# Delta-rule layer: exponentials and norm factors spread over partitions by way of DRAM, one pool limit for two kinds of tiles, keys ahead of queries

## The chip, the cores and the metric

The kernel runs on one core of a Trainium2 chip. The metric is the device time of one execution in microseconds (us). An execution is profiled by the hardware; the profile's span runs from the first to the last instruction.

## What is computed

One inference step of a 4-layer hybrid encoder for 512 prompt rows and 64 sample rows (576 columns in all) of width 1024. Layer 0 mixes by pooling, layer 1 by a gated delta rule, layer 2 by stick-breaking attention, layer 3 by pooling again, and a feed-forward part with a short causal convolution stands behind each mixer. The change touches the delta-rule layer alone:

```
qkv, z, a, b = split(h @ w_in); qkv = silu(causal_dwconv(qkv))          # 8 heads, head size 128
q = l2norm(q) * DK**-0.5; k = l2norm(k); beta = sigmoid(b)
g = -exp(a_log) * softplus(a + dt_bias)                                 # decay, one number per head and row
gc = cumsum(g) within a chunk
m = (k*beta) @ k.T * exp(gc_i - gc_j) below the diagonal                # per chunk and head
u, w = triangular_solve(I + m, [v*beta, k*beta*exp(gc)])
attn = (q @ k.T) * exp(gc_i - gc_j); qg = q * exp(gc); kg = k * exp(gc_last - gc)
for each chunk: v_new = u - w @ s; o = qg @ s + attn @ v_new; s = s*exp(gc_last) + kg.T @ v_new
o = rmsnorm(o, norm_w) * silu(z);  y = o @ w_out
```

## The kernel before, in words

All instructions go through a small planner. Each piece of work is a generator (a task) with a priority; it yields the tiles, buffers or events that it needs, and the planner, with a cost for each instruction and a due time for each tile, picks which task goes on. What comes out is one fixed order per engine, and every engine, the queue SP that issues all DMAs too, works in this program order. So an instruction that waits holds everything behind it on its engine. Since one helper issues everything, all rows of the profile bear the line L26; tiles are told apart by their names (a, b, d, h, p, q, r, t are pools of buffers; p is PSUM; dn_... are constants of this layer).

In the delta layer (`dn`) the planner has these tasks, for each of 8 heads:

- projections: for k, q, v and z of every head 48 matmuls (128x288, weights split in a high and a low part) on PE, in the order that the string `order` of the table TN gives (`k4` is the key of head 4). `conv` follows a k, q or v: POOL writes three columns of the old state ahead of the data and copies the last three columns out, DVE multiplies and adds, ACT takes tanh, DVE adds.
- `mat(h)`: the gram matrix of the key (PE), its diagonal (DVE), a power for the key's norm (POOL), decay factors by a small matmul (`bank`) and exponential (ACT), the product M (DVE), and seven stores of M to DRAM (SP). M has the class 'M', of which two tiles may be alive.
- `inverse(g)`: the triangular inverses of 32x32 blocks for four heads at a time, 31 steps of two POOL instructions. Group 0 waits for the matrices of heads 0 to 3, group 1 for those of heads 4 to 7.
- `merge(h)`: loads inverse blocks from DRAM, puts them together to U (class 'U', two tiles alive).
- `prep_rec(h)`: the masked products of q and k, and eg, the exponential of the cumulated decay of head h on all 128 partitions: `bank(h,None)` on PE (two matmuls, weights dn_idr) and two exponentials on ACT.
- `rec(h)`: the recurrence over the chunks, head after head. At its end the output o is normed: squares (ACT), sums over partitions (PE, ten matmuls with ones), a factor r[128,5] (DVE, then a power on POOL), the spread of these 576 factors over 128 partitions by five matmuls (ten instructions) against the identity (c_ident,t), and two multiplications (DVE, a<-p,dn_nw,a).
- `z_post(h)` multiplies o by silu(z), and the output projection (weights h, moving data b) takes all eight heads.

Of the kernel before, what the change touches and what calls it, by code (L numbers as in the profile page):

```python
# [9 lines left out]
F32 = mybir.dt.float32  # L10
F32R = mybir.dt.float32r
BF16 = mybir.dt.bfloat16
AF = mybir.ActivationFunctionType
ALU = mybir.AluOpType
# [22 lines left out]
class Flow:  # L37
# [213 lines left out]
TN={'mat': 2,  # L251
 'inv': 3,
 'merge': 5,
 'prep': 10,
 'rec': 2,
 'cv': 6,
 'M': 2,
 'tu': 4,
 'tu_': 2,
 'mg': 3,  # L260
 'U': 2,
 'v': 2,
 'vs': 2,
 'pr': 4,
# [7 lines left out]
 'pv': 4,  # L272
 'pz': 6,
 'w': 8,
 'order': 'k0 q0 q1 k1 k2 q2 k3 q3 v2 v0 v1 v3 k4 q4 k5 k6 q6 k7 q5 q7 z1 z0 z2 z3 v5 v4 v6 v7 z4 z5 z7 z6',
 'pa': 3,
 'pb': 2,
 'pc': 7,
# [11 lines left out]
class Step:  # L290
# [890 lines left out]
    def dn(self,l,st,nst,gnext):  # L1181
        nc=self.nc; I=self.I; O=self.O; mm=self.E.matmul; T_=self.E.transpose; V=self.V; A=self.A; G=self.G; S=self.S; f=self.f
# [5 lines left out]
        nw=c1([128,1],"nw"); mhalf=c1([128,5],"mhalf"); idr=c1([128,8],"idr",F32R)  # L1188
        cst=c1([128,3],"cst"); mc=c1([128,1],"mc")
        tok=c1([128,5,72],"tok")  # L1190
        bE=c1([128,5,8],"bE"); ngc=c1([128,5,8],"ngc"); beta=c1([128,5,8],"beta"); nbe=c1([128,5,8],"nbe"); ekg=c1([128,5,8],"ekg")
        gh=[None]
        cc=[slice(128*c,128*c+128) for c in range(4)]; sm=slice(512,576); ss=slice(SO,SO+64)
        blocks=[(128*b,128*b+128) for b in range(4)]+[(512,576)]
        def prep():
# [15 lines left out]
        def ab_post(P):  # L1211
            rb=self.rb[st]
            yield [f"{st}:rb0",f"{st}:rb1"]
            f.free(self.acc[st])
            yield [("a",3)]
            Yt=self.a(); t_=self.a(); Ft=self.a()
            Y=Yt[:40,:NT]; t=t_[:40,:NT]; F=Ft[:,:NT]
            self.lnexp()
            A.activation(mc[:40],cst[:40,2:3],AF.Exp)
            V.tensor_scalar(out=mc[:40],in0=mc[:40],scalar1=-1.0,scalar2=None,op0=ALU.mult)  # L1220
            G.memset(F,0.0)
            yield [P[0],P[1],rb[:,:NT]]
            for h,p in enumerate(P):
                a,b=HALF[h]
                V.tensor_tensor(out=Y[:,a:b],in0=p[:40,:HW],in1=rb[:40,a:b],op=ALU.mult)
            f.free(*P)
            V.tensor_scalar(out=Y,in0=Y,scalar1=cst[:40,0:1],scalar2=cst[:40,1:2],op0=ALU.mult,op1=ALU.add)
            yield [Y]
            A.activation(t,Y,AF.Abs)
            A.activation(t,t,AF.Exp,scale=-1.0)  # L1230
            A.activation(t,t,AF.Ln,bias=self.one[:40])
            yield [t]
            V.scalar_tensor_tensor(out=Y,in0=Y,scalar=0.0,in1=t,op0=ALU.max,op1=ALU.add)
            V.tensor_scalar(out=Y,in0=Y,scalar1=mc[:40],scalar2=None,op0=ALU.mult)
            V.tensor_copy(F[32:40],Y[32:40])
            for a,b in blocks:
                V.tensor_tensor_scan(out=F[0:8,a:b],data0=self.ones[0:8,:b-a],data1=Y[0:8,a:b],initial=0.0,op0=ALU.mult,op1=ALU.add)
                V.tensor_scalar(out=F[64:72,a:b],in0=F[0:8,a:b],scalar1=F[0:8,b-1:b],scalar2=-1.0,op0=ALU.subtract,op1=ALU.mult)
            yield [("a",1)]
            g=gh[0]=self.a(F32R)  # L1240
            G.memset(g[:,:NT].bitcast(F32),0.0)
            V.tensor_copy(g[0:8,:NT],F[0:8])
            V.tensor_tensor(out=g[32:40,:NT],in0=F[0:8],in1=g[0:8,:NT].bitcast(F32),op=ALU.subtract)
            f.free(Yt,t_)
            yield [F,("p",1)]
            p=self.p()
            for i,(a,b) in enumerate(blocks): T_(p[:b-a,72*i:72*i+72],F[0:72,a:b],self.ident[:72,:72])
            yield [p]
            V.tensor_copy(tok[:,0:4],p[:,:288].rearrange("p (a b) -> p a b",b=72))
            V.tensor_copy(tok[:64,4],p[:64,288:360])  # L1250
            f.free(p,Ft)
            V.tensor_tensor(out=bE,in0=tok[:,:,0:8],in1=tok[:,:,32:40],op=ALU.add)
            V.tensor_scalar(out=ngc,in0=tok[:,:,0:8],scalar1=-1.0,scalar2=None,op0=ALU.mult)
            yield [bE]
            A.activation(beta,tok[:,:,32:40],AF.Exp)
            A.activation(nbe,bE,AF.Exp)
            A.activation(ekg,tok[:,:,64:72],AF.Exp)
            yield [ekg]
            V.tensor_scalar(out=beta,in0=beta,scalar1=0.5,scalar2=None,op0=ALU.mult)
            V.tensor_scalar(out=nbe,in0=nbe,scalar1=-1.0,scalar2=None,op0=ALU.mult)  # L1260
            f.fire(f"{st}:dec")
# [109 lines left out]

        def mat(h):
            k=kq[h][:,0]
            yield [k[:,:579],("a",1,"M"),("p",2),("t",1)]
            M=self.a(cls="M"); r=self.s([128,5],F32,"t",8)
            p=self.p(); q=self.p()
            G.memset(r,1.0)
            for c in range(4): mm(p[:,cc[c]],k[:,cc[c]],k[:,cc[c]],start=True,stop=True)
            mm(q[:64,:64],k[:,ss],k[:,ss],start=True,stop=True)
            yield [p,q[:64,:64],r,"@V"]  # L1380
            for c in range(4): V.scalar_tensor_tensor(out=M[:,cc[c]],in0=p[:,cc[c]],scalar=1.0,in1=self.ident,op0=ALU.mult,op1=ALU.mult,accum_out=r[:,c:c+1])
            V.scalar_tensor_tensor(out=M[:64,sm],in0=q[:64,:64],scalar=1.0,in1=self.ident[:64,:64],op0=ALU.mult,op1=ALU.mult,accum_out=r[:64,4:5])
            V.tensor_scalar(out=r,in0=r,scalar1=4e-6,scalar2=None,op0=ALU.add)
            V.reciprocal(out=rk2[:,h],in_=r)
            G.tensor_tensor(out=r,in0=r,in1=mhalf,op=ALU.pow)
            yield [f"{st}:dec",("p",1)]
            p2=self.p()
            G.memset(M[64:128,sm],0.0)
            bank(h,self.mpos,p2,q,64)
            yield [r,rk2[:,h]]  # L1390
            V.tensor_tensor(out=nbk[:,h],in0=nbe[:,:,h],in1=rk2[:,h],op=ALU.mult)
            V.tensor_tensor(out=vsc[:,h],in0=beta[:,:,h],in1=r,op=ALU.mult)
            f.free(r)
            f.fire(f"{st}:kn{h}")
            yield [p2,q[:64,64:128],"@A"]
            for c in range(4): A.activation(M[:,cc[c]],p2[:,cc[c]],AF.Exp,scale=-1.0,bias=bE[:,c,h:h+1])
            A.activation(M[:64,sm],q[:64,64:128],AF.Exp,scale=-1.0,bias=bE[:64,4,h:h+1])
            f.free(p2)
            yield [M[:,:NT],"@V"]
            for c in range(4): V.scalar_tensor_tensor(out=M[:,cc[c]],in0=p[:,cc[c]],scalar=rk2[:,h,c:c+1],in1=M[:,cc[c]],op0=ALU.mult,op1=ALU.mult)  # L1400
            V.scalar_tensor_tensor(out=M[:64,sm],in0=q[:64,:64],scalar=rk2[:64,h,4:5],in1=M[:64,sm],op0=ALU.mult,op1=ALU.mult)
            f.free(p,q)
            g=h//4; o=18*(h%4)
            if g not in dM: dM[g]=self.dram([72,32,32])
            d=dM[g]
            yield [M[:,:NT]]
            for b in range(4):
                S.dma_start(out=d[o:o+16].rearrange("(c b) i j -> b i c j",b=4)[b],
                    in_=M[32*b:32*b+32,:512].rearrange("p (c j) -> p c j",j=128)[:,:,32*b:32*b+32])
            for b in range(2): S.dma_start(out=d[o+16+b],in_=M[32*b:32*b+32,512+32*b:544+32*b])  # L1410
            Mt[h]=self.dram([128,NT]); S.dma_start(out=Mt[h],in_=M[:,:NT])
            f.free(M)
            f.fire(f"{st}:M{h}")
# [90 lines left out]
        def prep_rec(h):  # L1504
# [3 lines left out]
            yield [("a",2,"pr"),("a",1,"eg"),("p",2),("d",1,"ks"),("t",1)]  # L1508
            at=self.a(cls="pr"); eg=self.a(cls="eg"); kg=self.a(cls="pr"); kgs=self.d("ks")[:64]; gl=self.s([128,5],F32,"t",8)
            p=self.p(); q=self.p()  # L1510
            bank(h,self.mneg,p,q,0)
            yield [p,q,"@A"]
            for c in range(4): A.activation(at[:,cc[c]],p[:,cc[c]],AF.Exp,bias=ngc[:,c,h:h+1])
# [4 lines left out]
            yield [p,q,"@V"]  # L1518
            V.tensor_tensor(out=at[:,:512],in0=p,in1=at[:,:512],op=ALU.mult)
            V.tensor_tensor(out=at[:64,sm],in0=q[:64,:64],in1=at[:64,sm],op=ALU.mult)  # L1520
            yield [at]
            bank(h,None,p,q,0)
            yield [p,q,"@A"]
            A.activation(eg[:,:512],p,AF.Exp)
            A.activation(eg[:,sm],q[:,:64],AF.Exp)
            yield [eg]
            for b in range(4): T_(p[:,cc[b]],k[:,cc[b]],self.ident)
            T_(q[:64,:128],k[:,ss],self.ident)
            G.tensor_copy(gl[:,0:4],eg[:,127:512:128]); G.tensor_copy(gl[:,4:5],eg[:,575:576])
# [9 lines left out]
        def rec(h):  # L1539
# [7 lines left out]
            for c in (4,0,1,2,3):  # L1547
# [3 lines left out]
                if s is not None:  # L1551
                    yield [s,ks,("p",1),("d",1,"rr")]
                    p=self.p()
# [42 lines left out]
            sq=self.a(cls="eg")  # L1596
            A.activation(sq[:,:NT],o[:,:NT],AF.Square)
            q=yield from sums(sq,512)
            f.free(sq)
            yield [("t",1)]  # L1600
            r=self.s([128,5],F32,"t",8)
            V.scalar_tensor_tensor(out=r,in0=q[:,:5],scalar=1.0/128,in1=eq[:,h],op0=ALU.mult,op1=ALU.add)
            G.tensor_tensor(out=r,in0=r,in1=mhalf,op=ALU.pow)
            yield [r,("p",1)]
            p=self.p()
            for i in range(4): mm(p[:,cc[i]],r[:,i:i+1].to_broadcast([128,128]),self.ident,start=True,stop=True)
# [8 lines left out]
        def z_post(h):  # L1615
# [25 lines left out]
                dno[h]=t  # L1641
                f.fire(f"{st}:o{h}")
            return g
        f.lim.update({k:TN[k] for k in ('cv','M','tu','tu_','mg','U','v','vs','pr','eg','ks','o_','S','rr')})
        def k_(h):
            if h: proj(8+h,qk_post(h,0),TN['pk'])
            else: first(qk_post(0,0))
# [390 lines left out]
```

## Time and profile before

| | |
|---|---|
| runs | 2484.01, 2489.79, 2485.27 us; median 2485.27 |
| profiled execution | 2487.87 us, its span 2486.1 us |
| PE busy | 2440.4 us, 98% of the span |
| DVE, ACT, POOL busy | 77%, 52%, 15% |
| mean granted TensorE clock | 0.995 |

The delta layer takes the stretch from about 450 to 880 us of the span. A granted clock of 1.00 is 2.4 GHz and 0.50 is 1.2 GHz. The chain that ended last lies on PE for 88% of the span.

### The profile page before, as it was taken

Reading aid. Unit: us, or ns where it says so; the run is one execution under the profiler, and the core shown is the slowest. Engines: PE = TensorE matmul, PEld = TensorE weight load, DVE = VectorE, ACT = ScalarE, POOL = GpSimd, SP = SyncE. Lnnn points to the kernel's source line nnn. Section 1 sums busy time; section 2 is a strip of 40 time slices with the busy share of each in tenths; the row PEclk is TensorE's granted clock in tenths of the full one; section 3 lists DMA queues with packets and bytes.
Section 4 is the critical chain, followed back from the end, with each engine's and each line's share of the span. In section 5 each row is a group of like instructions: output and inputs, shape, how many; then the busy total and the mean of one; then the engine's idle time right before and its main releaser. Section 6 shows DMA issues by size and latency. Waiting matters only on the chain.

```text
span 2486.1 us, 46793 instructions
## 1 busy us (share of the span) xinstructions
PE 2440.4 (98%) x18385; PEld 2381.6 (96%) x18385; DVE 1904.6 (77%) x3695; ACT 1282.5 (52%) x2419; POOL 373.1 (15%) x750
## 2 busy tenths in 40 slices
PE   8999999998999999999999999999999999999998
PEld 7999999998999999999999998899999999999998
DVE  6888877887556478877886777778777788977775
ACT  6445544544344344444556677644444466544445
POOL 0000000138431101000000322200000011100000
PEclk9999999999999999999999999999999999999999
DMA  4323323332321221323334122222223231323231
GB/s 111 88 86 102 95 80 97 103 96 62 82 64 50 86 87 52 103 85 94 94 109 128 49 88 65 92 77 78 85 87 101 85 111 49 91 76 94 86 102 57
DMA packets 349056, 212.92 MB, mean 86 GB/s; under 512 B 30298, under 2 KB 341210, under 8 KB 348836
## 3 DMA queue, kind: packets, MB, share of 16 engines
q1 hardware_dynamic: 348836, 209.93, 28.9%
q8 instruction: 145, 2.38, 0.4%
q14 instruction: 75, 0.61, 0.1%
HBM read 192.41 MB, written 17.47 MB: 84 GB/s over the span
## 4 chain that ended last, share of the span: by engine, by line
PE 88%; DVE 4%; issue 3%; POOL 3%; DMA 1%; ACT 1%; SPq 0%; DVEq 0%; POOLq 0%; ACTq 0%
PE p L26 88%; DVE a L26 2%; DVE h L26 1%; POOL h L26 1%; POOL q L26 1%; ACT a L26 1%; DMA b<-in_x_prompt_dram 0%; DVE r L26 0%; DVE b L26 0%; POOL a L26 0%; DMA a<-in_cache_sb_k_dram 0%; ACT b L26 0%; POOL t L26 0%; POOL dn_so L26 0%; SPq L26 0%
## 5 line engine op out<-in xcount | busy, mean ns | idle before, releaser
L26 PE MATMUL p<-xh,h 128*128 128x288 f32 x4992 | 1061.5, 300 | 4.6 <-DVE h L26 4.4
L26 PEld LDWEIGHTS p<-xh,h 128*128 128x128 f32 x4992 | 820.9, 189 | 10.1 <-DVE h L26 4.8
L26 PE MATMUL p<-xl,h 128*128 128x288 f32 x2496 | 720.3, 296 | 0.0
L26 ACT ACTIVATE h<-r 128x512 fp32r<-128x512 f32 (+1 forms) x688 | 499.6, 747 | 411.6 <-PE p L26 327.3
L26 PE MATMUL p<-b,h 128*128 128x288 f32 x4992 | 677.9, 296 | 4.9 <-DVE b L26 2.3
L26 PEld LDWEIGHTS p<-b,h 128*128 128x128 f32 x4992 | 666.2, 189 | 8.1 <-DVE b L26 3.8
L26 DVE TENSOR_TENSOR h<-r,h 128x512 fp32r<-128x512 f32 (+1 forms) x688 | 571.5, 840 | 43.3 <-ACT h L26 41.8
L26 PEld LDWEIGHTS p<-xl,h 128*128 128x128 f32 x2496 | 472.8, 189 | 0.5
L26 DVE TENSOR_TENSOR a<-p,a 128x288 f32<-128x288 f32 (+4 forms) x662 | 269.5, 446 | 204.9 <-PE p L26 190.7
L26 PE MATMUL p<-a,h 128*128 128x288 f32 x2448 | 347.6, 295 | 4.6 <-DVE h L26 3.9
L26 PEld LDWEIGHTS p<-a,h 128*128 128x128 f32 x2448 | 331.8, 188 | 6.3 <-DVE h L26 4.8
L26 POOL COPY so<-a 128x2 f32<-128x2 f32 x176 | 98.1, 587 | 1488.6 <-DVE a L26 1488.6
L26 ACT ACTIVATE a<-a 128x512 f32<-128x512 f32 (+7 forms) x358 | 192.4, 559 | 130.6 <-DVE a L26 109.9
L26 ACT ACTIVATE q<-p 128x288 f32<-128x288 f32 x272 | 111.6, 410 | 168.4 <-PE p L26 165.0
L26 DVE SCALAR_TENSOR_TENSOR a<-a,fcw,a 128x578 f32<-128x578 f32 x176 | 144.2, 819 | 6.8 <-ACT a L26 1.7
L26 ACT ACTIVATE b<-a 128x576 fp32r<-128x576 f32 x96 | 65.4, 682 | 87.4 <-DVE a L26 87.3
L26 ACT ACTIVATE xh<-a,gains 128x288 fp32r<-128x288 f32 (+2 forms) x128 | 66.3, 531 | 70.2 <-DVE a L26 69.7
L26 DVE TENSOR_TENSOR a<-p,q 128x288 f32<-128x288 f32 (+2 forms) x204 | 66.6, 355 | 46.5 <-PE p L26 46.5
L26 ACT ACTIVATE a<-p 128x448 f32<-128x448 f32 (+5 forms) x149 | 64.8, 454 | 71.7 <-PE p L26 54.4
L26 POOL TENSOR_TENSOR a<-a,a 128x512 fp32r<-128x512 f32 (+1 forms) x64 | 68.2, 1065 | 220.7 <-DVE a L26 202.4
L26 DVE TENSOR_TENSOR r<-r 128x512 f32<-128x512 f32 x136 | 94.4, 694 | 4.1
L26 PE MATMUL p<-a,a 128*128 128x128 f32 (+6 forms) x656 | 94.4, 284 | 1.1 <-ACT b L26 0.8
(192 smaller groups left out, 2457.2 us busy)
## 6 DMA issues: line engine op xcount, KB each, us to landing
r<-in_ffn_w_up_dram SPq DMA_DIRECT2D x176, 512.0 KB
r<-in_ffn_w_down_dram SPq DMA_DIRECT2D x80, 512.0 KB
r<-in_dn_w_in_dram SPq DMA_DIRECT2D x32, 512.0 KB
r<-in_sb_w_qkv_dram SPq DMA_DIRECT2D x24, 512.0 KB
d<-a SPq DMA_DIRECT2D x24, 288.0 KB
a<-d SPq DMA_DIRECT2D x16, 288.0 KB
r<-in_ffn_w_down_dram SPq DMA_DIRECT2D x16, 256.0 KB
r<-in_dn_w_out_dram SPq DMA_DIRECT2D x8, 512.0 KB
```

Of the source, the lines that this page charges most:

```text
L26: r = f(*a, **k)
```

## The change

Four things change, all in the delta layer. First, the exponential of the cumulated decay is taken once for the eight heads on 8 partitions and stored to DRAM (`eD`); `prep_rec` loads a head's row, repeated over 128 partitions, in place of two matmuls and two exponentials. Second, for heads 0 to 6 the norm factors r are stored to DRAM in the order of the rows (640 elements of four bytes) and loaded back, repeated over 128 partitions, in place of the five matmuls against the identity; one multiplication of 576 columns takes the place of two (512 and 64). Head 7 keeps the matmuls. Third, M and U share the class 'U', of which four may be alive, in place of two and two. Fourth, the projections have another order.

```diff
- 'M': 2,
- 'U': 2,
+ 'U': 4,
- 'order': 'k0 q0 q1 k1 k2 q2 k3 q3 v2 v0 v1 v3 k4 q4 k5 k6 q6 k7 q5 q7 z1 z0 z2 z3 v5 v4 v6 v7 z4 z5 z7 z6',
+ 'order': 'k0 k1 q0 q1 k2 k3 q2 q3 v0 v1 k4 k5 q4 k6 k7 q5 q6 q7 v2 v3 z0 z1 v4 v5 z2 z3 v6 v7 z4 z5 z7 z6',
 ...
-        gh=[None]
+        gh=[None]; eD=self.dram([8,NT])
 ...
+            A.activation(t_[0:8,:NT],F[0:8],AF.Exp)
+            yield [t_[0:8,:NT]]
+            S.dma_start(out=eD,in_=t_[0:8,:NT])
 ...
         def mat(h):
-            yield [k[:,:579],("a",1,"M"),("p",2),("t",1)]
-            M=self.a(cls="M"); r=self.s([128,5],F32,"t",8)
+            yield [k[:,:579],("a",1,"U"),("p",2),("t",1)]
+            M=self.a(cls="U"); r=self.s([128,5],F32,"t",8)
 ...
         def prep_rec(h):
+            S.dma_start(out=eg[:,:NT],in_=eD[h:h+1].to_broadcast([128,NT]))
 ...
-            yield [at]
-            bank(h,None,p,q,0)
-            yield [p,q,"@A"]
-            A.activation(eg[:,:512],p,AF.Exp)
-            A.activation(eg[:,sm],q[:,:64],AF.Exp)
-            yield [eg]
+            yield [at,eg[:,:NT]]
 ...
         def rec(h):
             q=yield from sums(sq,512)
-            f.free(sq)
             yield [("t",1)]
             r=self.s([128,5],F32,"t",8)
             V.scalar_tensor_tensor(out=r,in0=q[:,:5],scalar=1.0/128,in1=eq[:,h],op0=ALU.mult,op1=ALU.add)
             G.tensor_tensor(out=r,in0=r,in1=mhalf,op=ALU.pow)
+            if h<7:
+                f.free(q)
+                yield [r]
+                dr=self.dram([5,128])
+                with nc.allow_non_contiguous_dma(reason="640 factors"): S.dma_start(out=dr.rearrange("b p -> p b"),in_=r)
+                f.free(r)
+                yield [dr]
+                S.dma_start(out=sq[:,:NT],in_=dr.rearrange("(o b) p -> o (b p)",o=1)[:,:NT].to_broadcast([128,NT]))
+                yield [sq[:,:NT],"@V"]
+                V.scalar_tensor_tensor(out=o[:,:NT],in0=sq[:,:NT],scalar=nw,in1=o[:,:NT],op0=ALU.mult,op1=ALU.mult)
+                f.free(sq)
+                oo[h]=o
+                f.fire(f"{st}:on{h}")
+                return
+            f.free(sq)
```

How the planner's order moves is read from the two programs. On POOL, in the first inverse, each step is a pair q<-h,h and h<-h,q; the memset and copy of three columns and the copies to dn_so belong to the convolution of a key or value. Before, the convolution of the key of head 4 (tile a_6964) stands behind the sixteenth step, and its copies to dn_so behind the eighteenth:

```order
L26 TENSOR_TENSOR h_6622<-h_6622,q_6626 72x16x16
L26 MEMSET a_6964 128x3
L26 COPY a_6964<-dn_st 128x3
L26 TENSOR_TENSOR q_6626<-h_6621,h_6622 72x255
L26 TENSOR_TENSOR h_6622<-h_6622,q_6626 72x15x17
L26 TENSOR_TENSOR q_6626<-h_6621,h_6622 72x252
L26 TENSOR_TENSOR h_6622<-h_6622,q_6626 72x14x18
L26 COPY dn_so<-a_6964 128x3 x2
```

With the change that key's pieces (tile a_6799) stand behind the thirteenth and fourteenth step:

```order
L26 TENSOR_TENSOR h_6535<-h_6535,q_6539 72x19x13
L26 MEMSET a_6799 128x3
L26 COPY a_6799<-dn_st 128x3
L26 TENSOR_TENSOR q_6539<-h_6534,h_6535 72x252
L26 TENSOR_TENSOR h_6535<-h_6535,q_6539 72x18x14
L26 COPY dn_so<-a_6799 128x3 x2
```

So the same key stands three to four steps earlier in the inverse, and the inverse itself begins earlier in the layer, because the keys of heads 2 and 3 come sooner.

At the norm of head 0, PE before works on the spread of the factors (t_8023 is r of head 0) between the gram matrix of head 7 and the next sums:

```order
L26 MATMUL p_7991<-b_6140 128x128 x4
L26 MATMUL p_7992<-b_6140 64x64
L26 MATMUL p_8052<-c_ident,t_8023 128x128 x4
L26 MATMUL p_8000<-c_ident,t_8023 128x64
L26 MATMUL p_8062<-ones,a_7896 128x1 x4
L26 MATMUL p_8062<-ones,a_7896 64x1 x2
```

With the change the two rows with c_ident,t are gone there, and SP has the store of r (t_7931) and the load of the spread factors (into a_7919) in their place, ahead of the loads for the next merge and the state of head 2 (d_8142):

```order
L26 DMA a_7940<-d_129 128x576
L26 DMA r_7960<-in_dn_w_in_dram 128x8x128
L26 DMA d_7973<-t_7931 128x5x1
L26 DMA a_7919<-d_7973 128x576
L26 DMA a_8085<-d_6508 32x4x32 x2
L26 DMA a_8085<-d_6508 32x32
L26 DMA a_8086<-d_7225 32x4x32 x4
L26 DMA a_8086<-d_7225 32x32 x2
L26 DMA a_8087<-d_7223 32x4x32 x4
L26 DMA a_8087<-d_7223 32x32 x2
L26 DMA a_8088<-d_6508 64x4x64
L26 DMA d_8142<-in_state_dn_dram 128x128
```

In SP's order the load follows its store directly, and it can't go before the store has landed. On DVE the multiplication that uses the load stands seven rows behind the factor, with steps of the next head's recurrence (d<-p,dn_nbk,a) on either side:

```order
L26 SCALAR_TENSOR_TENSOR t_7931<-p_7921,dn_eq 128x5
L26 SCALAR_TENSOR_TENSOR a_7906<-a_7905,dn_cw,a_7906 128x579 x3
L26 TENSOR_TENSOR a_7797<-a_7797,p_7913 64x64
L26 TENSOR_TENSOR a_7797<-a_7797,p_7912 128x512
L26 SCALAR_TENSOR_TENSOR d_7995<-p_7984,dn_nbk,a_6813 128x128
L26 SCALAR_TENSOR_TENSOR a_7906<-a_7905,a_7906 128x579
L26 TENSOR_TENSOR a_7798<-a_7798,p_7913 128x512
L26 SCALAR_TENSOR_TENSOR d_8025<-d_7975,t_6265,p_8021 128x128
L26 SCALAR_TENSOR_TENSOR a_7567<-a_7919,dn_nw,a_7567 128x576
L26 SCALAR_TENSOR_TENSOR d_8046<-p_8037,dn_nbk,a_6813 128x128
```

The multiplication (a_7567) stands ahead of d_8046, the next chunk's step of head 1, which waits behind it.

## Rows read from the trace of the kernel before

**Rows 1.** The page's busy times and its DMA queue (packets, MB, share).

```profile
PE 2440.4 (98%) x18385; PEld 2381.6 (96%) x18385; DVE 1904.6 (77%) x3695; ACT 1282.5 (52%) x2419; POOL 373.1 (15%) x750
...
q1 hardware_dynamic: 348836, 209.93, 28.9%
```

**Rows 2.** Busy time by stretch: length, engines (instructions), granted clock, DMA share, GB/s.

```profile
550.00:600.00 50.00, 44.14 (x318) 43.20 (x317) 35.22 (x66) 18.95 (x34) 45.73 (x76) 0.93 0.24 61
...
650.00:700.00 50.00, 48.23 (x379) 44.74 (x379) 26.23 (x51) 20.73 (x56) 35.15 (x63) 1.00 0.15 37
...
585.40:592.20 6.80, 5.66 (x25) 4.98 (x26) 4.89 (x19) 2.54 (x6) 6.27 (x13) 0.50 0.00 0
872.10:875.50 3.40, 3.40 (x16) 3.40 (x15) 2.83 (x7) 2.57 (x7) 0.00 (x0) 0.50 0.09 24
```

**Rows 3.** PE's timeline: start, duration, instruction, [idle before <-releaser].

```profile
580.25 0.43 PE L26 MATMUL p<-xh,h 128*128 128x288 f32 x2
586.54 1.22 PE L26 MATMUL p<-b 128*128 128x128 f32 x4 [5.86 <-DVE b L26]
...
608.00 0.30 PE L26 MATMUL p<-a,dn_idr 128*128 128x64 f32 x1 [0.80 <-DVE a L26]
...
614.93 1.33 PE L26 MATMUL p<-b 128*128 128x128 f32 x9 [0.92 <-DVE b L26]
```

**Rows 4.** The timeline of ACT and DVE at the same place.

```profile
585.01 0.69 ACT L26 ACTIVATE a<-a 128x579 f32<-128x579 f32 x1 [4.33 <-POOL dn_so L26]
...
585.73 0.76 DVE L26 SCALAR_TENSOR_TENSOR b<-a,a 128x579 f32<-128x579 f32 x1 [1.41 <-ACT a L26]
```

**Rows 5.** POOL's timeline in the first inverse.

```profile
550.95 0.54 POOL L26 TENSOR_TENSOR q<-h,h 72x31 f32<-72x31 f32 x1 [3.96 <-issue]
...
584.79 0.31 POOL L26 COPY dn_so<-a 128x3 f32<-128x3 f32 x2
...
590.31 1.65 POOL L26 TENSOR_TENSOR t<-t,dn_mhalf 128x5 f32<-128x5 f32 x1
...
593.86 0.55 POOL L26 TENSOR_TENSOR q<-h,h 72x207 f32<-72x207 f32 x1
594.48 2.17 POOL L26 TENSOR_TENSOR h<-h,q 72x207 f32<-72x207 f32 x1
...
607.19 0.25 POOL L26 TENSOR_TENSOR h<-h,q 72x31 f32<-72x31 f32 x1
```

**Rows 6.** Groups of PE instructions by shape, 450 to 880 us (busy us, mean ns).

```profile
L26 PE MATMUL p<-c_ident,t 128*128 128x128 f32 x64 | 8.8, 281 | 0.3 <-POOL t L26 0.3
...
L26 PE MATMUL p<-c_ident,t 128*128 128x64 f32 x16 | 2.7, 248 | 0.0
```

**Rows 7.** PE's timeline at a spread of factors and at a bank for eg.

```profile
667.37 1.33 PE L26 MATMUL p<-c_ident,t 128*128 128x128 f32 x10
668.53 1.16 PE L26 MATMUL p<-ones,a 128*128 128x1 f32 x10
...
675.21 0.51 PE L26 MATMUL p<-a,dn_idr 128*128 128x512 f32 x2
675.65 0.43 PE L26 MATMUL p<-d,a 64*64 64x128 f32 x2
```

**Rows 8.** PE's timeline at the layer's end.

```profile
867.06 1.23 PE L26 MATMUL p<-c_ident,t 128*128 128x128 f32 x10
868.10 1.04 PE L26 MATMUL p<-b,h 128*128 128x288 f32 x6
...
870.73 0.40 PE L26 MATMUL p<-b,h 128*128 128x288 f32 x1 [1.37 <-ACT b L26]
871.52 1.35 PE L26 MATMUL p<-b,h 128*128 128x288 f32 x6 [0.39 <-DVE b L26]
```

**Rows 9.** Pieces of the chain that ended last: start, duration, what.

```profile
545.53 1.43 DMA d<-a
...
547.00 3.95 issue
```

More of the change, by code (lines that the diff above doesn't have):

```diff
@@ L1643, in z_post @@
             return g
-        f.lim.update({k:TN[k] for k in ('cv','M','tu','tu_','mg','U','v','vs','pr','eg','ks','o_','S','rr')})
+        f.lim.update({k:TN[k] for k in ('cv','tu','tu_','mg','U','v','vs','pr','eg','ks','o_','S','rr')})
         def k_(h):
```

## The prediction

> **What bounds the kernel now.** I read the page's busy times first. PE works for 98% of the span, the other engines for 77% and less [rows 1], so time can go in three ways only: work taken from PE, stalls of PE, and a lower clock under PE's work. The table by stretches shows where PE isn't full within the delta layer: 44.1 of 50 us between 550 and 600, 48.2 between 650 and 700 [rows 2]. In 550 to 600 POOL is busy for 45.7 us, more than PE: that is the first inverse. PE's timeline gives the stall: its last projection matmuls start at 580.25 and the next row, the gram matrix of the key of head 4, starts at 586.54 after 5.86 us of idle time, released by DVE; smaller ones of 0.80 and 0.92 follow at 608.00 and 614.93 [rows 3].
>
> Who is late is seen by going back from that gram. DVE's last step of the convolution starts at 585.73 and waited for ACT; ACT's tanh starts at 585.01 and waited 4.33 us for POOL's tile dn_so [rows 4]. On POOL the two copies to dn_so stand between the steps of the inverse and start at 584.79 [rows 5]. They need nothing that is late; they stand in line. So PE waits for POOL, and DVE, which is named, does not bind. The stall has a second price: from 585.4 to 592.2 the granted clock is 0.50, which is 1.2 GHz, after the idle time ahead of it, and 6.8 us at half speed lose 3.4 us of work [rows 2]. The layer's end has the same form: 1.37 and 0.39 us of idle time at 870.73 and 871.52 [rows 8], then 3.4 us at 0.50, which lose 1.7 us [rows 2].
>
> **The change, part by part.** The sum is made on the profiled execution, 2487.87 us (span 2486.1 and 1.8 us around it); it lies 2.6 us above the median of the runs shown, 2485.27.
>
> *Matmuls taken out.* The spread of a head's factors starts at 667.37 and the next row on PE at 668.53: 1.16 us [rows 7]. At the end it is 867.06 to 868.10, 1.04 us [rows 8]. The groups confirm the count, 64 and 16 instructions for eight heads, 11.5 us busy with overlap [rows 6]. Seven heads at 1.1 us are 7.7 us. The bank for eg starts at 675.21 and the next row at 675.65: 0.44 us [rows 7], 3.5 us for eight heads. Together 11.2 us of work leave PE in a stretch in which PE is nearly full. Bounds: 11.2 if PE has other work in each place, near 0 if PE then only waits for the recurrence (a rival below). I take 11.2, since the projections of v and z are there as filling work. The sixteen exponentials that leave ACT, and on DVE two multiplications from PSUM that become one of 576 columns (0.76 us by the same shape with 579 columns [rows 4]), lie beside PE and are counted as nothing.
>
> *Loads of eg.* They are issued 5 to 10 us of PE work ahead of their use. The nearest load of this size, 288 KB from DRAM into the inverse's tile, has 3.95 us from issue to POOL's first step [rows 5, 9]. The early issue hides it: 0. Without this cover it would be at most 3.95 us a head.
>
> *Norm factors by way of DRAM.* The trip is the power on POOL (1.65 us [rows 5]), a store, and a load that waits for it. A small store of M took 1.43 us in the chain [rows 9], but it has 32 pieces and this one 640 of four bytes. On average a packet took 0.289 x 16 x 2486.1 / 348836 = 33 ns of a DMA engine [rows 1]; 640 over 16 engines add 1.3 us. So the estimate is 1.4 + 1.3 for the store and 4.0 for the load, 6.7 us, with 5.4 (no cost of pieces) as lower bound. Above, by the 1.43 us for 32 pieces if it all were their cost, 29 us; that is far off, since a 288 KB load needs 3.95, so I lean to the packets' mean. Against it stands the PE work between factor and multiplication in the new order, priced by the trace's rows: 8.2, 8.9, 7.9, 11.2, 8.7, 9.5 and 8.5 us for heads 0 to 6, less the power. That leaves 6.3 to 9.6 us for a trip of 6.7. Behind the waiting multiplication DVE holds the next head's step of the recurrence, so lateness there goes through to PE. On SP the load of head 1 stands also behind the stores of the second inverse. Behind SP's waiting store stand the merge's loads and a state load, not due for some us. I count 1.5 us, from 0 to 10.
>
> *Order and one limit.* The keys come sooner, so the inverse begins earlier, and the keys of heads 4 to 6 stand earlier between its steps, in POOL's order after 14 steps instead of 18 for head 4. This doesn't remove the wait, since POOL needs the same time: from 550.95 to 607.44, 56.5 us [rows 5]. Counted from the inverse's start, PE comes to the gram of head 4 after 23.8 us of work where POOL, by its own rows, lets it go at about 25.8; head 5 at 32.9 against 39.7, the sums of q of head 4 at 41.0 against 49, head 6 at 48.6 against 57 to 58. These lags don't add, as a stall shifts all that comes behind: the total is the largest, about 9 us, in four or five pieces, with 0 to 3.4 us of lowered clock. Before it was 5.86 + 0.80 + 0.92 [rows 3] and 3.4 of clock, 11.0. So 9 to 12.4 against 11.0: I take 0, from -11 (no lag left, if POOL's long steps, as the one of 2.17 us [rows 5], all ran at 0.55) to +5. The common limit of four only lets a matrix start while no merge holds a tile; what it moves is in this order already.
>
> *The layer's end.* Before, 6 matmuls of the output projection stand behind the last spread (and two transposes), and PE then waits [rows 8]. With the change the projection of the last z ends sooner, and 54 matmuls stand between this spread and the first one that needs head 7. At some 0.13 us a matmul (48.23 us for 379 [rows 2]) they cover 7 us, and the chain needs 870.73 - 868.10 = 2.6 us from the spread's end, or 3.4 with the last idle time [rows 8]. So 1.37 + 0.39 us of idle time and 1.7 us of clock go: -3.4, from -3.5 to 0.
>
> Sum: -11.2 - 3.4 + 0 + 1.5 = -13.1, so 2474.8 us on the profiled execution, and 2472 against the median.
>
> **Rivals.**
>
> *POOL binds harder.* Five waits for POOL in the inverse, each long enough to lower the clock as the one at 585.4 did, cost 9.4 and some 6.8 us of clock, 16.2 against 11.0. For it: a POOL step of the same shape took 2.17 us instead of 0.55 while DVE multiplied [rows 5], so new work on DVE can lengthen the inverse. Against it: the pieces are smaller than 5.86, and only that one brought the clock down. It gives +5 on the sum, 2477. The Trainium skill (SBUF — State Buffer, "Who interferes with whom") says that a DVE instruction with two SBUF inputs and a GpSimd instruction that reads SBUF exclude each other for the whole instruction. The trace agrees in the 2.17 us; by this rule the change's multiplications, which now read both inputs from SBUF, and one more convolution in the inverse's time would add up to 3 us.
>
> *The freed PE time is only waited out.* The recurrence is a chain over PE, DVE and ACT; if it sets the pace from 660 to 860, matmuls taken out of PE leave idle time. It would give 2485, no change. Against it: between 650 and 700 PE waits for 1.8 of 50 us [rows 2], so the chain keeps up with a full PE. For it: once the projections are used up, nothing else fills.
>
> *The trip is late (slower).* The gain is 13.1 us, or 1.9 for each of seven heads. If the store takes 4 us more than I estimate, the load lands 4 us late, DVE stands before the next head's step, and PE with its filling work loses some 2.4 us and 1.7 of clock as at the end [rows 8]: 4.1 x 7 = 29 us more, or 2500. It decides from about 1.9 us of PE's time lost a head, a trip of some 9 us. For it: the store has twenty times the pieces of any row that I priced it by. Against it: the distances of 6.3 us and more. The Trainium skill (DMA: Bandwidth & Descriptors, "Rules for kernel authors") speaks against the change: a strided last dimension becomes one descriptor for each element. No run here shows how long 640 of them take; by this page the trip would be longer than by the small store's row alone.
>
> **How the numbers follow.** No change means within 0.2%, 5 us, which is about what a measurement of this kernel can tell. The forecast's case has 0.62 (2460 to 2480), POOL binding harder 0.14 (2474 to 2484, two thirds of it still faster), the freed time waited out 0.11 (2482 to 2489), the late trip 0.13 (2490 to 2510). Faster: 0.62 + 0.10 = 0.72; no change 0.11 + 0.03 = 0.14; slower 0.14 with the worst of the second. Time 2472; the range 2460 to 2488 leaves out the late trip and a little below. The lower end is the case that the inverse's stalls go altogether: -11.2 - 3.4 - 11.0 = -25.6 on 2485.27, 2460.
>
> **What would show it.** In the profile after: PE busy some 11 us less and eight heads' matmuls with c_ident,t down to one head's ten instructions. The two exponentials of eg gone from ACT and no wait of DVE for eg. PE's idle time in the inverse in several pieces that name DVE or ACT with POOL behind them, together near 9 us. No idle time of more than 0.5 us at the layer's end, and no stretch of 0.50 clock there. DVE's a<-a,dn_nw,a with waits for DMA below 1 us a head; waits of 2 us and more there, with PE idle behind them, prove me wrong, and so would PE's busy time falling by 11 us with as much idle time gained between 660 and 860.

## The result and the profile after

The changed kernel takes 2526.17 us (median of 4 runs, 2524.08 to 2530.38), against 2486.57 us for the kernel before in the same comparison: ratio 1.0158, 95% interval 1.0145 to 1.0171. It is slower by 39.6 us where 13 us less were forecast. The profiled span is 2522.3 us, 36.2 more than before.

The page's busy times of the changed kernel answer to [rows 1]:

```profile
PE 2445.5 (97%) x18299; PEld 2384.8 (95%) x18299; DVE 1903.0 (75%) x3688; ACT 1277.3 (51%) x2404; POOL 371.9 (15%) x750
```

PE has 86 instructions less and is yet busy 5.1 us longer. The table by stretches of the changed kernel shows why (length, engines in the order of [rows 2], granted clock, DMA share, GB/s):

```profile
600.00:650.00 50.00, 46.33 (x333) 43.15 (x334) 28.26 (x82) 18.55 (x37) 29.34 (x63) 0.90 0.36 90
...
700.00:750.00 50.00, 39.27 (x273) 35.97 (x272) 20.32 (x39) 17.71 (x45) 6.89 (x13) 0.86 0.42 72
...
800.00:850.00 50.00, 41.07 (x289) 37.68 (x289) 23.77 (x48) 18.80 (x49) 4.28 (x14) 0.93 0.22 54
850.00:900.00 50.00, 41.29 (x306) 39.71 (x305) 20.09 (x39) 15.44 (x32) 2.54 (x2) 0.90 0.35 101
```

Before, PE worked for 47.9 us and more in each of these four stretches, at a clock of 0.97 to 1.00. Now it stands for about 9 to 11 us in three of them, and the clock is low behind each longer stall. Counted over the trace from 440 to 960 us, PE's idle time rises from 13.6 to 45.6 us (+32). Stretches at half clock, less the part in which PE was idle anyway, lose about 19.7 us of work in place of 4.5 (+15). With 11.2 us of matmuls gone that makes +36, which is the difference of the spans.

PE's timeline in the changed kernel, six of the eight stalls of more than 1 us (the other two are 3.81 us at 707.48 and 4.52 us at 842.94):

```profile
571.08 1.22 PE L26 MATMUL p<-b 128*128 128x128 f32 x4 [3.23 <-DVE b L26]
603.67 1.62 PE L26 MATMUL p<-b 128*128 128x128 f32 x6 [4.29 <-DVE b L26]
677.57 0.80 PE L26 MATMUL p<-d,a 128*128 128x128 f32 x2 [5.72 <-DVE d L26]
735.47 0.66 PE L26 MATMUL p<-d,b 128*64 128x128 f32 x2 [6.82 <-DMA d<-in_state_dn_dram]
819.70 0.77 PE L26 MATMUL p<-d,b 128*128 128x128 f32 x2 [4.41 <-DVE d L26]
887.55 0.80 PE L26 MATMUL p<-d,a 128*128 128x128 f32 x2 [8.37 <-DVE d L26]
```

The first two are at the first inverse, as before. The other six are new, and all are steps of the recurrence (p<-d,...). The chain of waits of the changed kernel says what they wait for (start, duration, what):

```profile
689.51 1.17 POOL t L26
...
690.70 11.07 DMA d<-t
...
701.83 3.70 DMA a<-d
...
725.15 10.19 DMA d<-in_state_dn_dram
...
869.36 12.09 DMA d<-t
...
881.50 4.89 DMA a<-d
...
886.41 0.82 DVE a L26
887.23 0.27 DVE d L26
```

`d<-t` is the store of the 640 norm factors. It takes 11 to 12 us here, counted from the start of the issuing instruction. By the trace's events, counted from that instruction's end, the seven stores land 7.6 to 11.1 us after their issue, 9.4 in the median. The load behind it takes 3.7 and 4.9 us, about the 4.0 that was expected. The power is done at 690.7, and DVE gets its factors at 705.5. At the end of the chain the multiplication (DVE a, 886.41) and the recurrence's step behind it (DVE d, 887.23) follow the load, and PE starts at 887.55 after 8.37 us of idle time. The state load at 725.15 waits for no factor; it was issued 0.5 us behind a store of factors and takes 10.19 us. The waits of DVE for the tile dn_nw in the changed kernel sum it up:

```profile
L26 DVE SCALAR_TENSOR_TENSOR a<-a,dn_nw,a x7: 817/819/819, 676.4 to 886.4; 128x576 f32<-128x576 f32 x7
...
  DMA a<-d: 36.2, 6
```

Six of seven multiplications found their load late, by 36.2 us together, and with DVE stood all that is queued behind it.

### The profile page after: what moved, and what is told of

It reads as the page before. It is cut to its first block, busy times and chain, and to the rows that moved or that the text cites. A ratio compares the mean times of both kernels' runs of the same rounds, so it can differ in the third digit from the quotient of the medians.

```text
span 2522.3 us, 46632 instructions
## 1 busy us (share of the span) xinstructions
PE 2445.5 (97%) x18299; PEld 2384.8 (95%) x18299; DVE 1903.0 (75%) x3688; ACT 1277.3 (51%) x2404; POOL 371.9 (15%) x750
## 4 chain that ended last, share of the span: by engine, by line
PE 85%; DVE 4%; issue 3%; DMA 3%; POOL 2%; ACT 1%; SPq 0%; DVEq 0%; POOLq 0%; ACTq 0%
PE p L26 85%; DVE a L26 2%; DVE h L26 1%; DMA d<-t 1%; POOL q L26 1%; DMA a<-d 1%; POOL h L26 1%; ACT a L26 1%; DMA d<-in_state_dn_dram 1%; POOL t L26 0%; DVE r L26 0%; DVE b L26 0%; DMA a<-in_cache_sb_k_dram 0%; POOL dn_so L26 0%; ACT b L26 0%
## 5 line engine op out<-in xcount | busy, mean ns | idle before, releaser
L26 DVE TENSOR_TENSOR a<-p,a 128x288 f32<-128x288 f32 (+5 forms) x662 | 269.4, 446 | 208.4 <-PE p L26 193.8
L26 ACT ACTIVATE a<-a 128x64 f32<-128x64 f32 (+7 forms) x359 | 193.2, 559 | 137.8 <-DVE a L26 129.4
L26 DVE TENSOR_TENSOR r<-r,r 128x512 f32<-128x512 f32 x136 | 93.5, 688 | 2.5
```

The source lines that it names most:

```text
L26: r = f(*a, **k)
```

## The experiments

The theory was that the store in 640 pieces of four bytes is what costs the time, by itself and by what it holds up. The first rival was that the new order and the common limit do it, by the stalls at the inverse; the second that a store and a load in series are late whatever their pieces.

**e1: the factors on PE again.** `rec` as before, the rest of the change stays.

```diff
-            if h<7:
...
-                return
...
             yield [r,("p",1)]
             p=self.p()
             for i in range(4): mm(p[:,cc[i]],r[:,i:i+1].to_broadcast([128,128]),self.ident,start=True,stop=True)
```

> The changed kernel with one part undone: the norm factors are spread by matmuls as before, the exponentials of the decay still by way of DRAM, the common limit and the new order stay. Theory (the store in 640 pieces): in the changed kernel this store landed 7.6 to 11.1 us after its issue, against 2.7 that I had estimated, and it holds up DVE and what is queued behind it; without it the time falls to 2486.6 - 3.5 (bank matmuls gone) - 3.4 (layer's end) = about 2480, 2472 to 2488. Rival (the order): the new order and the common limit cost the time, by stalls of PE behind the inverse (3.23 and 4.29 us with a lowered clock in the changed kernel's trace) and by what follows from them; then the time stays above 2505.

Measured: 2486.77 us, ratio 1.000 (0.9991 to 1.001). The 40 us are gone, so order and limit don't cost them. But the 6.9 us that I expected from the rest aren't there either. The bank's matmuls are gone, and yet PE is busy for 2440.4 us as before: from 440 to 960 us the low clock costs 7.8 us of work in place of 4.5.

**e2: this part alone.** The kernel before with the factors by way of DRAM.

```diff
+            if h<7:
...
+                with nc.allow_non_contiguous_dma(reason="640 factors"): S.dma_start(out=dr.rearrange("b p -> p b"),in_=r)
...
+                S.dma_start(out=sq[:,:NT],in_=dr.rearrange("(o b) p -> o (b p)",o=1)[:,:NT].to_broadcast([128,NT]))
...
+                V.scalar_tensor_tensor(out=o[:,:NT],in0=sq[:,:NT],scalar=nw,in1=o[:,:NT],op0=ALU.mult,op1=ALU.mult)
...
```

> The kernel before with one part of the change: the norm factors of heads 0 to 6 by way of DRAM, nothing else. Theory (the store in 640 pieces): seven trips of about 14 us each where 6 to 9 us are covered; 2486.6 - 7.7 + 7 x 6.5 = about 2524, 2510 to 2540. Rival (the order): this part gains its matmuls, about 2479, at most 2486.

Measured: 2539.18 us, ratio 1.0213 (1.0196 to 1.023), 52 us more, worse than the whole change. The theory holds, 15 us above its 2524 and at the upper end of its range.

**e3: the store that nobody reads.**

```diff
             G.tensor_tensor(out=r,in0=r,in1=mhalf,op=ALU.pow)
+            if h<7:
+                yield [r]
+                dr=self.dram([5,128])
+                with nc.allow_non_contiguous_dma(reason="640 factors"): S.dma_start(out=dr.rearrange("b p -> p b"),in_=r)
             yield [r,("p",1)]
```

> The kernel before, with the store of the 640 factors added for heads 0 to 6; nobody reads what it stores, the factors are spread by matmuls as before. Theory (pieces, and they hold up the whole DMA queue): transfers issued behind it land late, the next head's state among them, some 8 to 10 us after issue instead of 1.5 to 3; two to four stalls of PE of 3 to 7 us with a lowered clock, 2495 to 2510. Rival (only the reader of the store waits): 2486.6 within 4 us, and state loads at their old 1.5 to 3 us.

Measured: 2499.83 us, ratio 1.0054 (1.0039 to 1.0069). So 13 us are lost though no instruction waits for what is stored. The chain of waits of e3 shows two of the next heads' state loads late, where the eight of the kernel before took 1.9 to 4.1 us:

```profile
772.46 7.33 DMA d<-in_state_dn_dram
...
823.76 9.14 DMA d<-in_state_dn_dram
```

and PE's timeline what comes of it:

```profile
832.94 0.43 PE L26 MATMUL p<-d,b 128*64 128x128 f32 x2 [3.91 <-DMA d<-in_state_dn_dram]
```

So the pieces hold up transfers that are issued behind them. Three of PE's stalls name a state load: those of 2.16 and 3.91 us the two shown, the one of 1.81 us a load that was issued 0.6 us ahead of its store. The clock falls behind two of them, and the rival on the reader alone is out. An unread store in few pieces wasn't run, so how much of the 13 us the moved order takes isn't shown.

**e4: 128 pieces instead of 640.**

```diff
-                dr=self.dram([5,128])
-                with nc.allow_non_contiguous_dma(reason="640 factors"): S.dma_start(out=dr.rearrange("b p -> p b"),in_=r)
+                dr=self.dram([128,5])
+                S.dma_start(out=dr,in_=r)
```

> The changed kernel, with the factors stored as they lie, five to a partition: 128 pieces of 20 bytes in place of 640 of four, and loaded back by the same load; the factors then stand in another order along the rows, so the normed output is another, all work and waits are the same. Theory (the number of pieces): the store lands 1.5 to 2.5 us after its issue, the trip takes some 6 to 7 us, and the forecast's sum holds: about 2473, 2466 to 2483. Rival (a store and a load in series are late whatever their pieces): still above 2505.

Measured: 2480.69 us, ratio 0.9975 (0.9964 to 0.9986): 45 us less than the changed kernel, from the same bytes, the same load and the same two DMAs in series. The queue's own waits show it. In the changed kernel, 640 to 900 us (us in total, times, longest):

```profile
SPq L26 <- DMA d<-t: 51.1, 6, 9.7
```

In e4:

```profile
SPq L26 <- DMA d<-t: 8.6, 4, 4.4
```

By the events these stores land 1.07 us after issue in the median. This settles that the cause is how the store is cut, not its bytes and not the two DMAs in series. The number of pieces alone it is not: a weight load of 512 KB (in_dn_w_in) has 1024 pieces of 512 bytes and mostly lands 3.4 to 4.7 us after issue in the changed kernel. Four bytes alone it need not be either: the load of the norm's 128 weights, in 128 pieces of four bytes, lands within 1.7 us in the kernel before. Whether it is the two together, or that it is a store whose neighbours in DRAM come from different partitions, no run separates. The Trainium skill (DMA: Bandwidth & Descriptors, "Rules for kernel authors") has the rule, one descriptor for each element of a strided last dimension; the trace of the changed kernel agrees, with some 640 packets of four bytes behind each such store, and these runs give this one a price, 9.4 us.

**e5: the right order in 5 pieces.** PE transposes the factors, and rows of 512 bytes are stored.

```diff
-                f.free(q)
-                yield [r]
+                yield [r,"@A"]
+                T_(q[:5,128:256],r,self.ident)
+                rt=sq[:5,:128]
+                yield [q[:5,128:256],"@A"]
+                A.activation(rt,q[:5,128:256],AF.Copy)
+                f.free(q,r)
+                yield [rt]
                 dr=self.dram([5,128])
-                with nc.allow_non_contiguous_dma(reason="640 factors"): S.dma_start(out=dr.rearrange("b p -> p b"),in_=r)
-                f.free(r)
+                S.dma_start(out=dr,in_=rt)
```

> The changed kernel with the right order of the factors in few pieces: PE transposes r to 5 partitions, ACT copies it to SBUF, and the store has 5 pieces of 512 bytes; load and multiplication as in the changed kernel. Theory (pieces): the store lands within 2 us, the time is that of the kernel with 128 pieces, 2480.7, and some 0.2 us a head for the transposition: 2482, 2476 to 2487. Rival (PE waits in its order for the power on POOL, as it did before): stalls of about 1 us a head with a lowered clock now and then, 2488 or more.

Measured: 2476.99 us, ratio 0.9951 (0.9936 to 0.9966). It does what the changed kernel does, and is faster than before by 0.5%. These stores land after 1.04 us in the median. SP's wait for them falls to this row, seven waits of 1.5 us in the mean, one of 3.9:

```profile
SPq L26 <- DMA d<-a: 10.5, 7, 3.9
```

**e6 and e7: POOL's pieces of the convolution elsewhere,** in e5 and in the kernel before.

```diff
-            G.memset(C[:,0:3],0.0); G.tensor_copy(C[:,515:518],cst_[:,t::24])
+            V.memset(C[:,0:3],0.0); A.activation(C[:,515:518],cst_[:,t::24],AF.Copy)
...
-            G.tensor_copy(so[:,0:3,t],C[:,512:515]); G.tensor_copy(so[:,3:6,t],C[:,579:582])
+            A.activation(so[:,0:3,t],C[:,512:515],AF.Copy); A.activation(so[:,3:6,t],C[:,579:582],AF.Copy)
```

> The kernel of the transposed store, with the small pieces of the convolution (a memset, a copy of three columns, two copies to dn_so) taken from POOL: the memset on DVE, the copies on ACT. Theory (POOL's line at the first inverse is what PE waits for): the stalls of 3.2 and 4.3 us and most of the lowered clock behind them go, 8 us of idle time and 7 of clock; 13 us less than the kernel of the transposed store, about 2469, 2462 to 2476. Rival (DVE, which the trace names at these stalls, is itself behind): within 4 us of the kernel of the transposed store.

> The kernel before with the same pieces taken from POOL and nothing else. Theory (POOL's line): the stall of 5.86 us, the smaller ones and 3.4 us of clock go, 11 us less at most: 2477, 2473 to 2482. Rival (DVE is behind): 2486.6 within 4.

Measured: e6 2479.62 us, ratio 0.9965 (0.9952 to 0.9978), no gain over e5; e7 2495.11 us, ratio 1.0032 (1.0022 to 1.0041), slower than before. Both of e7's expectations missed, and e6 came out at its rival's time. My reading of [rows 4, 5] was wrong in its size. PE's timeline of e7 still has the stall at the gram of head 4, 2.2 us shorter than in [rows 3], and a second one has grown:

```profile
584.16 1.23 PE L26 MATMUL p<-b 128*128 128x128 f32 x4 [3.65 <-DVE b L26]
...
606.84 1.39 PE L26 MATMUL p<-b 128*128 128x128 f32 x6 [2.95 <-DVE b L26]
```

DVE's timeline of the kernel before has the row that I left out. Its three multiplications end at 584.31, only 0.7 us before the tanh of [rows 4] could start:

```profile
580.86 3.45 DVE L26 SCALAR_TENSOR_TENSOR a<-a,dn_cw,a 128x579 f32<-128x579 f32 x3
```

They take 1.15 us each beside POOL's steps, where the same three took 0.82 each with POOL idle:

```profile
513.22 2.52 DVE L26 SCALAR_TENSOR_TENSOR a<-a,dn_cw,a 128x579 f32<-128x579 f32 x3
```

So DVE was nearly as late as POOL, and in e7 the same tanh waits for DVE in place of POOL:

```profile
582.36 0.69 ACT L26 ACTIVATE a<-a 128x579 f32<-128x579 f32 x1 [4.04 <-DVE a L26]
```

A wait that is put down to the last comer says little about the second last. In the kernels with the new order, POOL holds PE by another way as well. ACT's timeline of e5 shows the copy of the finished inverse, which waited for POOL's last step, ahead of the tanh that the gram at 603.05 needs:

```profile
599.56 1.97 ACT L26 ACTIVATE h<-h 72x1024 f32<-72x1024 f32 x1 [4.97 <-POOL h L26]
601.43 0.68 ACT L26 ACTIVATE a<-a 128x579 f32<-128x579 f32 x1
```

In e6 that copy comes later, at 608.87, with no stall of PE behind it, and PE's two stalls at the inverse shrink from 3.23 and 4.66 to 1.17 and 1.75 us:

```profile
573.50 1.42 PE L26 MATMUL p<-b 128*128 128x128 f32 x10 [1.17 <-DVE b L26]
...
578.12 0.30 PE L26 MATMUL p<-a,dn_idr 128*128 128x64 f32 x1 [1.75 <-DVE a L26]
```

So POOL's line did hold PE there. But PE's idle time from 440 to 960 us is 12.3 us in e5 and in e6: in e6 others take its place, three waits for state loads of 0.84 to 1.37 us among them. What makes e7 slower than before isn't settled: moving the pieces changes the planner's order all through the layer, the low clock costs 8.6 us of work in place of 4.5, and it is longest at the layer's end (10.2 us from 869.9).

**e8, e11, e12: what order and limit are worth,** once the trip is short. All three have e5's DRAM paths; e8 has the old order and the old limits, e11 the new order and the old limits, e12 the old order and the new limit. With the old limits `mat` takes its class 'M' again.

```diff
- 'U': 4, 'order': 'k0 k1 q0 q1 k2 k3 ...'            # e5
+ 'M': 2, 'U': 2, 'order': 'k0 q0 q1 k1 k2 q2 ...'     # e8
+ 'M': 2, 'U': 2, 'order': 'k0 k1 q0 q1 k2 k3 ...'     # e11
+ 'U': 4, 'order': 'k0 q0 q1 k1 k2 q2 ...'             # e12
```

> The kernel before with both ways by DRAM (the exponentials of the decay; the factors with the transposed store), the old order of projections and the old limits. If the new order costs more at the inverse (15 to 17 us of idle time and clock against 11) than it gives at the layer's end (1.8): about 2486.6 - 11.2 + 1.4 = 2477, 2472 to 2481, faster than the transposed store with the new order. Rival (order and limit are worth nothing either way): equal to it within 3.

> The kernel of the transposed store with the old limits (two matrices, two U) and the new order of projections. Old order and old limits together took 2489.4 where the new ones took 2477.0. If the common limit of four is what the 12 us need, this one takes 2486 or more; if the order of projections is, it takes 2477 within 4.

> The counterpart: the transposed store with the common limit of four and the old order of projections. If the order is what the 12 us need: 2486 or more; if the limit is: 2477 within 4; 2480 to 2485 if it is both.

Measured: e8 2489.39 us, ratio 1.0006 (0.9996 to 1.0016); e11 2479.07, 0.9968 (0.9957 to 0.998); e12 2483.76, 0.9989 (0.9979 to 0.9999); e5 was 0.9951 (0.9936 to 0.9966). Neither expectation for e8 held. With the old order and limits the two DRAM paths gain nothing at all, though PE has the same 11 us less to do. In its profiled execution, which took 2495.20 us, PE's stalls of over 0.25 us from 440 to 960 us come to 20.0 us against 11.7 in e5, and its clock falls five times between 680 and 885. By the ratios the new order gives 9 us under either limit, clear of the intervals. The limit gives 4 us under either order, and there the intervals overlap.

**e10: the planner told the store's true time.**

```diff
+            if out.space == bass.MemoryType.DRAM and out.ap[-1][0] != 1:
+                self.clk["D"] += 7400
             end = self.clk["D"] + 900
```

> The changed kernel, in which the planner is told that the store in 640 pieces takes 7.4 us more and holds up the DMA engines for as long; the instructions are the same, their order isn't. If the harm was that the order counted on a fast store, the multiplications move back behind other work and most of the loss goes: 2490 to 2500. If the 640 pieces harm whatever stands around them (state and weight loads late, a recurrence that needs its output buffers), it stays above 2510.

Measured: 2494.73 us, ratio 1.0036 (1.0022 to 1.005). So 31 us of the changed kernel's time came from an order that counted on a store of 2 us. What this order doesn't take away is 8 us against the kernel before, and 18 against e5, whose store has few pieces. In e10's chain of waits a load for a merge and a state load, issued 1.0 and 0.5 us behind such a store, still take 12.70 and 10.69 us:

```profile
713.74 12.70 DMA a<-d
...
796.91 10.69 DMA d<-in_state_dn_dram
```

**e9: the planner told a longer time for POOL's steps,** in e5.

```diff
-                return 149 + 2.1 * n
+                return (149 + 2.1 * n) * (1.35 if out.shape[0] == 72 else 1)
```

> The kernel of the transposed store, in which the planner's price of an inverse step on POOL is raised by 35%; no instruction changes, only their order. Theory (what is left at the inverse comes from an order that trusts POOL to be faster than it is beside DVE): the stalls of 3.2 and 4.7 us and the 6.8 us of lowered clock shrink by half or more, 2477.0 - 6 = about 2471, 2465 to 2475. Rival (POOL's time is needed whatever the order, as nothing else is there to fill): within 3 us of 2477.

In e5's trace the 62 steps of the first inverse take 44.4 us, 38% more than the planner's formula gives; those of the second take 37.1, 15% more.

Measured: 2468.17 us, ratio 0.9924 (0.9909 to 0.9939), 9 us less than e5 and faster than both kernels of this study. PE's timeline of e9 has one longer stall left at the inverse:

```profile
567.25 1.42 PE L26 MATMUL p<-b 128*128 128x128 f32 x10 [1.56 <-DVE b L26]
```

and in its table by stretches, of an execution of 2464.12 us, the stretch from 550 to 650 us is nearly full, at full clock:

```profile
550.00:600.00 50.00, 47.14 (x357) 45.20 (x358) 42.88 (x105) 21.81 (x44) 43.22 (x72) 1.00 0.33 89
600.00:650.00 50.00, 50.00 (x386) 47.63 (x385) 35.54 (x75) 20.58 (x34) 34.28 (x72) 1.00 0.38 99
```

Its working instructions are those of e5 in kind, shape and number, only their order differs; the rival that POOL's time must be waited out in any order is wrong.

## Why the prediction was wrong

The step that failed is the price of the store: "640 over 16 engines add 1.3 us. So the estimate is 1.4 + 1.3 for the store". It measured 9.4 us in the median in place of 2.7, and with the 1.07 us of e4 as its fixed part the pieces cost 8.3 us in place of 1.3. I had taken the mean time of all packets in the kernel, 33 ns of one engine, for the price of a piece of four bytes; 9.4 us for 640 pieces over 16 engines are 235 ns each, the fixed part of the transfer included. And packet time could not have told it. In the changed kernel the store issued at 662.84 has its four-byte packets between 663.70 and 664.40, some 7 ns of an engine each:

```profile
DMA packets 656, 0.00 MB, mean 4 GB/s; under 512 B 656, under 2 KB 656, under 8 KB 656
...
q1 hardware_dynamic: 656, 0.00, 43.2%
```

From 664.40 to 671.80 no further packet of SP's queue is recorded (the one packet is of another queue, q8), and only then has the store landed and SP issues the load, at 671.89:

```profile
DMA packets 1, 0.02 MB, mean 2 GB/s; under 512 B 0, under 2 KB 0, under 8 KB 0
```

So the time lies between the last packet and the landing; what the store does there the traces don't show. The upper bound that I wrote down, 29 us, lay three times too high and my estimate three times too low, and I leant to the low end because a transfer of 288 KB takes 4 us. But that one has 72 pieces of 4 KB, and bytes were not the question.

The rival on the late trip had the right mechanism, place and point of decision, with a chance of 0.13. It lacked the second half: the store holds up the transfers behind it too. "Behind SP's waiting store stand the merge's loads and a state load, not due for some us" looked at SP's order alone; e3 shows that a load which SP issues at once is late as well, by up to 7 us.

The other steps, one by one:

- *Matmuls taken out, 11.2 us.* The instructions are gone as said (ten of `c_ident,t` are left, for head 7). Where the trip is short and the order new, PE's busy time falls: 2432.7 us in e4 and 2432.1 in e5 against 2440.4 [rows 1]. So 8 us of 11.2 show; more work at half clock takes the rest back, and in e5 the seven transposes.
- *Loads of eg at no cost.* No wait of PE names them in the changed kernel. No run has them by themselves, so that they cost nothing isn't shown apart.
- *Norm factors, 1.5 us.* Wrong, as told above. With 5 pieces the term is, if anything, too high: e5 lies 9.8 us below e1, which spreads the factors on PE, and 7.7 of matmuls were counted.
- *Order and limit, 0.* Wrong in the sum's form: it isn't a term by itself. The 11.0 that I set for the kernel before was 10.4, since PE stood for 1.1 of the 6.8 us at half clock [rows 2]. At the inverse e5 has some 8.6 us of idle time and 6 us lost to the clock, 14.6 against these 10.4, near the 16.2 of the rival "POOL binds harder". But without the new order the freed matmuls are waited out: e8 is the rival "the freed PE time is only waited out", and happens with the old order only.
- *The layer's end, -3.4.* The idle time is gone in e1, e4 and e5, and no row of more than 0.5 us stands there in them. The low clock went in e5, not in e1 and e4 (3.4 us at 0.50 from 839.4 and 834.0), each by one execution. So -1.8 to -3.4. In the changed kernel the last factors' late trip puts a stall of 8.37 us in its place.

With the store in 5 pieces the forecast sum of -13.1 us measures -10.7 (2476.99 against 2487.65 in that comparison). The sum is near for a kernel that moves its factors in few pieces, and this one doesn't. That it is so near is in part luck: the inverse was dearer by some 4 us, and the factors cheaper.

## What to carry to other kernels

Look at how a transfer is cut before its bytes: look for the last dimension that isn't contiguous, and if no row of the trace has a transfer of such pieces, let the range reach the far bound. The time that packets take is not a price for the time to landing. A slow transfer has two costs, the wait of its reader and the lateness of all that is issued behind it; a store that nobody reads tells the second by itself. Where a planner sets the order, a wrong price in its table can cost as much as the operation: a nearer price of POOL's steps gave 9 us with no working instruction changed, and a nearer price of the store took back 31 of the 49 us between the changed kernel and e5.

## What the runs showed of the hardware that I had not expected

A store of 640 elements of four bytes landed after 9.4 us in the median, one of the same 2560 bytes in 128 pieces after 1.07 us, and a weight load of 512 KB issued 1 us behind such a store of 640 after 13.2 us, where 3.4 to 4.7 us were usual in the changed kernel.

The granted clock can fall with no idle time of PE ahead of it. In e4 PE was busy throughout when it fell to 1.2 GHz at 834.0, behind a group of small matmuls, as the table by stretches shows:

```profile
831.50:834.00 2.50, 2.50 (x21) 2.21 (x21) 0.91 (x3) 1.38 (x3) 0.96 (x1) 1.00 0.02 7
834.00:837.40 3.40, 3.40 (x16) 3.40 (x16) 2.16 (x3) 0.42 (x2) 0.20 (x1) 0.50 0.11 23
```

In PE's timeline these are sums over partitions and steps of the recurrence with 64 and 128 columns:

```profile
832.67 0.48 PE L26 MATMUL p<-d,d 64*128 64x128 f32 x2
833.09 0.43 PE L26 MATMUL p<-b,d 128*128 128x64 f32 x2
833.45 0.43 PE L26 MATMUL p<-a,d 64*128 64x64 f32 x2
833.82 0.47 PE L26 MATMUL p<-xh,h 128*128 128x288 f32 x1
```

So an order that gathers such steps can pay for it even where PE shows as busy: 1.7 us of work here. It isn't this one place. In ten of the fourteen traces (the changed kernel's, e1, e4 to e6, e8 to e12) the clock falls so between 440 and 960 us, fifteen times in all, each time behind twelve or more matmuls of sums over partitions (p<-ones,a). Most such groups, some sixteen in each of these traces, pass at full clock, so they alone don't settle it.
